# A streaming encoder step on one Trainium2 core: the head tables are made three pairs of blocks later, the planner is told of the weights' three places, and the weights' rounding is written behind a block's first step

## The chip, the core and the metric

The kernel runs on one core of one Trainium2 chip. Its engines run side by side, each through its own list of instructions in order: TensorE (PE in the profile) multiplies, VectorE (DVE), ScalarE (ACT) and GpSimd (POOL) do everything else, and SyncE (SP) issues most transfers. An engine whose next instruction waits for something stands still, with all that is queued behind it. The metric is the device time of one execution in microseconds.

## The reference

Two layers of an encoder run on 512 new frames and on 64 frames that continue a stream with 1024 cached frames; here they are 576 columns side by side. What matters of one layer:

```
h = rms_norm(x, norm_g);  proj = h @ w_in          # u, z, q, k, v, qi, ki, wi, z_a, g_p, g_a
br_pool = (pool_mix(u) * silu(z)) @ w_pool_out
q, k, qi, ki = rope(...)                           # rotary embedding
score = sum_h wi * relu(qi . ki);  keep the top 128 (new stream) or 256 (cached stream)
o = softmax(q k^T over the kept) v                 # 8 heads of 64
br_attn = (o * silu(z_a)) @ w_attn_out
x = x + (sigmoid(g_p) * br_pool + sigmoid(g_a) * br_attn) @ w_o
```

All of it is float32. The kernel reaches that accuracy with TensorE's faster fp32r format by splitting each operand in a rounded high part and the rest, and adding three products.

## The kernel before

**Blocks.** The weights come as 59 pieces of 128x1024 per layer. One piece makes one block: 8 steps of 6 matmuls over 288 columns (`step`, called by `product`, called by `block`). `ORDER` sets the blocks of a layer: 2 index queries, u0-u3 and z0-z3 (pooled branch), then four groups of two gates and one pooled output (gp0, gp1, po0, ..., gp6, gp7, po3), then k, q and v of four head pairs, za0-za3, ga0-ga7, four attention outputs and eight blocks wo0-wo7 of w_o.

**Weights.** SP loads a piece into one of three `raw` places. ScalarE writes the rounded part into the first half of a `whl` tile (three places) and minus the rounded part into the second half; GpSimd then issues a DMA that adds the raw piece to that second half (`split_to`). In block i `split_to(i + 3)` is written ahead of the block's matmuls, so ScalarE's two instructions for piece i+2 stand there. Their `whl` place is that of piece i-1, so they wait until TensorE has ended block i-1.

**Order.** The program is scheduled by hand: each engine's order is the order in which the code is written. A class `Plan` keeps for each engine the time at which it would be free by a table of costs. All work other than the blocks (attention units, transposes, selection) stands in generators. After every step `plan.pump()` asks which generator's next piece could run by the plan, and writes it there. So a cost or a wait that the plan does not know moves work to places where it is not ready. `Plan.slot` tells the plan when a place of a ring comes free for some rings, but not for `whl`.

**Head tables.** `head_tables()` loads the cosine and sine tables (two 288 KB loads on SP) into `tmp` tiles, and GpSimd multiplies each by the norm factors `Rt` into `Ct` and `St` (128x576 each). Blocks k and q use them. It is started at gp0.

**Attention.** For each head: logits into PSUM (`sm<-quart,qz` and `qzl`), minimum and mask on VectorE, exponential and normalising on ScalarE (`prob`), transposes on TensorE (`sm<-ident,prob`), rounding on ScalarE and rest on VectorE (`big`), values on TensorE (`sm<-big,quart`). PSUM has four `sm` places. The cached stream follows (`sample`): logits `sm<-big,qzs`, one exponential over 1088 columns, transposes `sm<-ident,quart`. In layer 0, block wo's output goes through `added`: two ScalarE instructions (rounded input of the next layer, square).

Of the kernel before, what the change touches and what calls it, by code (L numbers as in the profile page):

```python
# [11 lines left out]
F32R = mybir.dt.float32r  # L12
# [3 lines left out]
P = 128  # L16
# [30 lines left out]
UNITS = 3  # L47
FIRST_H = ()
LAG = (1, 2)
DMA_US = 3.0  # L50
WARM = 11
NORM_A = 0
# [12 lines left out]
class Plan:  # L65
# [77 lines left out]
    def run(self, eng, op, args, kw):  # L143
# [18 lines left out]
        if eng == "dma" or op == "dma_start":  # L162
            n = 1
            for k in outs[0].shape[1:]:
                n *= k
            late = DMA_US + 4 * outs[0].shape[0] * n / 180e3
        for x in outs:
# [48 lines left out]
    def start(self, gen, rank=1):  # L216
        item = [rank, len(self.todo), gen, None]
        self.todo.append(item)
        self.todo.sort(key=lambda x: x[0])
        self.step(item)  # L220
        return item
# [46 lines left out]
def encoder_step(ctx: ExitStack, tc: tile.TileContext, a: dict):  # L268
    nc = tc.nc
    plan = Plan()  # L270
# [5 lines left out]
    rot = ctx.enter_context(tc.tile_pool(name="rot", bufs=1))  # L276
# [7 lines left out]
    def tmp(n=T, dtype=F32):  # L284
        return rot.tile([P, 608], dtype, name="tmp", tag="tmp", bufs=NTMP)[:, :n]
# [16 lines left out]
    def ps_mm():  # L302
        return plan.slot("mm", 2, psum.tile([P, 2, 512], F32, name="mm", tag="mm", bufs=2), False)

    def ps_s(hold=False):
        return plan.slot("sm", 4, psum.tile([P, 512], F32, name="sm", tag="sm", bufs=4), hold)
# [22 lines left out]
    for l in range(DEPTH):  # L329
        pieces += [(l, j) for j in range(a["n_pieces"])]  # L330
    raw_of, split_of = {}, {}
    state = {"load": 0, "split": 0, "next": 0}

    def load_to(n):
        while state["load"] < min(n, len(pieces)):
            i = state["load"]
            l, j = pieces[i]
            raw_of[i] = raws()
            dma.dma_start(raw_of[i], a["w"][l, j])
            state["load"] += 1  # L340

    def split_to(n):
        while state["split"] < min(n, len(pieces)):
            i = state["split"]
            load_to(i + 1)
            x = raw_of.pop(i)
            w = rot.tile([P, 2, 1024], F32R, name="whl", tag="whl", bufs=3)
            act.copy(w[:, 0], x)

            act.activation(w[:, 1], x, AF.Copy, scale=-1.0)  # L350
            pool.dma_start(w[:, 1].bitcast(F32), x, accum_op=OP.add)
            plan.let(x)
            split_of[i] = w
            state["split"] += 1

    def split_first(i=0):

        load_to(i + 1)
        x = raw_of.pop(i)
        w = rot.tile([P, 2, 1024], F32R, name="whl", tag="whl", bufs=3)  # L360
        for c, eng in ((slice(0, 512), dve), (slice(512, 1024), pool)):
            act.copy(w[:, 0, c], x[:, c])
            eng.tensor_tensor(w[:, 1, c], x[:, c], w[:, 0, c].bitcast(F32), op=OP.subtract)
        plan.let(x)
        split_of[i] = w
        state["split"] = i + 1

    def weights():
        i = state["next"]
        state["next"] += 1  # L370
        split_to(i + 1)
        load_to(i + 4)
        w = split_of.pop(i)
        return w, i
# [60 lines left out]
    ps = ps_s()  # L435
# [3 lines left out]
    def step(ps, w, xh, xl, k, nk, off=0, parts=((0, 0, HT), (1, HT, T)), low=(False, True)):  # L439

        c = slice(off + k * P, off + (k + 1) * P)
        wh, wl = w[:, 0, c], w[:, 1, c]
        for s, t0, t1 in parts:
            cols = slice((k % 2) * T + t0, (k % 2) * T + t1)
            h, lo = xh[k // 2][:, cols], xl[k // 2][:, cols]
            o = ps[:, s, :t1 - t0]
            if False in low:  # L450
                pe.matmul(o, lhsT=wh, rhs=h, start=k == 0, stop=False)
                pe.matmul(o, lhsT=wh, rhs=lo, start=False, stop=False)
            if True in low:
                pe.matmul(o, lhsT=wl, rhs=h, start=False, stop=k == nk - 1)

    def product(ps, w, xh, xl, nk, off=0):
        for k in range(nk):
            step(ps, w, xh, xl, k, nk, off)
            plan.pump()

    def block(xh, xl, nk=8):
        w, i = weights()
        split_to(i + 3)
        ps = ps_mm()
        product(ps, w, xh, xl, nk)
        return ps

    class Entry:
# [29 lines left out]
        def first(self, k, x, ki_split):  # L498

            c = slice((k % 2) * T, (k % 2 + 1) * T)  # L500
            g = gains[:, self.l, k:k + 1]
            h = self.h[k // 2][:, c]
            if k in FIRST_H:
                dve.tensor_scalar(h, x, g, None, op0=OP.mult)
            else:
                act.activation(h, x, AF.Copy, scale=g)
            if k == 0:
                ki_split()
            dve.scalar_tensor_tensor(self.lo[k // 2][:, c], x, g, h.bitcast(F32), op0=OP.mult, op1=OP.subtract)
            self.rest.append(x)  # L510
            if k == 7:
                for i, x in enumerate(self.rest):
                    sq = tmp() if i else self.acc
                    act.activation(sq, x, AF.Square)
                    if i:
                        dve.tensor_tensor(self.acc, sq, self.acc, op=OP.add)
# [27 lines left out]
    def prepare_ki(l):  # L544
        rk = prob()
        rki = rk[:, :320].rearrange("p (k c) -> p k c", k=8)
        dma.dma_start(rk[:, :320], a["w_ki"][l])

        def ki_split():
            act.copy(kiw[:, :, 0:40], rki)  # L550
            (pool if l else dve).tensor_tensor(kiw[:, :, 64:104], rki, kiw[:, :, 0:40].bitcast(F32), op=OP.subtract)

        return ki_split

    def layer(l, x, arrive):
        xh, xl = x.h, x.lo
# [10 lines left out]
        w, n = weights()  # L567
        if l:
            split_to(n + 3)
# [8 lines left out]
        ps_k, ps_q0 = [ps_s(True) for _ in range(2)], ps_mm()  # L578
        lag = (0, 0) if l else LAG
        for k in range(8 + lag[1]):  # L580
# [30 lines left out]
        w, n = weights()  # L611
# [234 lines left out]

        def u_job(g):
            ps = block(xh, xl)
            ux = tmp(608)
            pool.memset(ux[:, 0:PST], 0.0)  # L850
# [96 lines left out]
        def po_job(m2):  # L947
            if m2 == 0:
                plan.finish(*mixes)
            w, n = weights()  # L950
            split_to(n + 3)
            for i in range(2):
                ps = ps_mm()
                product(ps, w, ah, al, 4, off=512 * i)
                pb = sgs.pop(2 * m2 + i)
                dve.tensor_tensor(halves(pb), ps[:, :, :HT], halves(pb), op=OP.mult)

                def go(pb=pb, m=2 * m2 + i):
                    yield lambda: need("dma", pb)
                    dma.dma_start(mp_d[l][m], pb)  # L960

                start(go(), 2)
            if m2 == 3:
                let(*ah, *al)
# [3 lines left out]
        def head_tables():  # L968
            Ct.append(rot.tile([P, T], F32, name="Ct", tag="acc", bufs=1))
            for raw, t in zip((table(2), table(3)), (Ct[0], St)):  # L970
                yield lambda: need("pool", raw)
                pool.tensor_tensor(t, raw, Rt, op=OP.mult)
# [150 lines left out]
        def attend():  # L1123
            yield lambda: {1, 2, 3} <= done
            for p in range(4):
                yield lambda: p in kv and p in q_there
                for e in range(2):
                    yield lambda: 2 * p + e < 2 + len(heads_done)
                    for j in (3, 2, 1, 0):
                        yield lambda: on_way[0] < UNITS and psum_free() and need("pe", kv[p], *qz[p]) and need("dve", room=ROOM)  # L1130
                        on_way[0] += 1
                        start(unit(p, e, j), 2)
                        logits_of[p] = logits_of.get(p, 0) + 1
                let(kv[p])
            let(macc)
            yield lambda: len(heads_done) == 8 and 4 in done
            yield from sample()
# [182 lines left out]
        for name, i in ORDER:  # L1320
            if name == "k" and i == 0:
                att = start(attend(), 3)
            if name == "gp" and i == 0:
                start(head_tables(), 2)
            jobs[name](i)
        plan.finish(sel)
# [14 lines left out]
        for m2 in range(4):  # L1341
            w, n = weights()
            split_to(n + 3)
            for i in range(2):
# [4 lines left out]
                ps = ps_mm()  # L1349
# [27 lines left out]
        for m in range(8):  # L1377
            residual(m + 1)
            if m == 3 and l + 1 < DEPTH:
                ki_split = prepare_ki(l + 1)  # L1380
# [4 lines left out]
            ps = block(mh, ml)  # L1385
# [57 lines left out]
        for s, t0, t1, starts in ((0, 0, CUT, (0, P, CUT - P)), (1, CUT, T, (CUT, T - P))):  # L1443
            for m in (6, 7):
                w, ps = wps[m - 6]
# [11 lines left out]
    ki_split = prepare_ki(0)  # L1457
# [7 lines left out]
    def arrive(k):  # L1465
        x.first(k, xt[k // 2][:, (k % 2) * T:(k % 2 + 1) * T], ki_split)
        if k == 7:
            plan.let(*xt)
        if k == 1:
            split_first()  # L1470
# [110 lines left out]
```

## Time and profile before

| | us |
|---|---|
| median of 3 runs | 920.47 (920.26 to 920.74) |
| the profiled execution | 921.1, its span 919.3 |
| TensorE busy | 894.8 (97% of the span) |
| VectorE busy | 668.3 (73%) |
| ScalarE busy | 593.2 (65%) |
| GpSimd busy | 202.1 (22%) |
| DMA by GpSimd's queue / by SP's queue | 59.78 MB / 100.08 MB |

The span runs from the first to the last instruction. Busy time of a pipelined TensorE counts a matmul from issue to result, longer than the distance at which the next may follow. "Idle before" in brackets is how long the engine stood still before the instruction, and what ended that.

### The profile page before, as it was taken

What the parts mean: (1) busy time and instruction counts of PE and PEld (TensorE: products, weight loads), DVE (VectorE), ACT (ScalarE), POOL (GpSimd) and SP (SyncE); (2) the same over time, 40 slices, a digit from 0 to 9 for tenths busy, and PEclk for the clock granted to TensorE, in tenths of its full rate; (3) what the DMA queues carried; (4) which work ended last, traced back from release to release, by engine and by line L of the source; (5) the groups of instructions that cost most, each with busy time, mean ns of one, the idle gap of its engine ahead of it and who ended that gap; (6) DMA issues with size and microseconds to landing.
All of it is one profiled execution on the core that took longest, in us unless ns stands there. A gap on an engine that the chain in (4) does not pass through costs nothing.

```text
span 919.3 us, 17403 instructions
## 1 busy us (share of the span) xinstructions
PE 894.8 (97%) x6613; PEld 881.4 (96%) x6613; DVE 668.3 (73%) x1554; ACT 593.2 (65%) x1056; POOL 202.1 (22%) x217
## 2 busy tenths in 40 slices
PE   8999999999999999999999999999999999999996
PEld 7999999999999999999999999999999999999995
DVE  6996899799896677362359779988989875755314
ACT  7556534588898975564537564446889988556642
POOL 3111211134432300112211121113443222011121
PEclk9999999999999999999999999999999999999998
DMA  7756587766555675779976667786655548648862
GB/s 266 187 140 164 134 214 189 173 161 160 125 145 147 179 199 150 186 202 240 263 191 175 154 151 163 191 203 180 165 139 133 157 124 221 189 135 222 236 146 104
DMA packets 54500, 160.97 MB, mean 175 GB/s; under 512 B 6736, under 2 KB 9040, under 8 KB 54416
## 3 DMA queue, kind: packets, MB, share of 16 engines
q0 software_dynamic: 16416, 59.78, 34.8%
q1 hardware_dynamic: 38000, 100.08, 32.2%
q8 instruction: 52, 0.85, 0.4%
q14 instruction: 32, 0.26, 0.1%
HBM read 85.37 MB, written 14.69 MB: 109 GB/s over the span
## 4 chain that ended last, share of the span: by engine, by line
PE 68%; DVE 14%; ACT 13%; issue 3%; DMA 1%; POOL 1%; SPq 0%; DVEq 0%; ACTq 0%; POOLq 0%
PE mm L262 57%; PE sm L262 11%; DVE tmp L262 6%; DVE quart L262 6%; ACT prob L262 4%; ACT whl L262 3%; ACT quart L262 2%; ACT qz L262 1%; ACT L262 1%; DVE big L262 1%; ACT tmp L262 1%; POOL tmp L262 1%; DMA raw<-in_w_dram 1%; DMA prob<-in_c_v_dram 1%; DVE prob L262 0%
## 5 line engine op out<-in xcount | busy, mean ns | idle before, releaser
L262 PE MATMUL mm<-quart,whl 128*128 128x288 f32 (+1 forms) x5568 | 780.4, 296 | 1.6 <-ACT quart L262 1.2
L262 PEld LDWEIGHTS mm<-quart,whl 128*128 128x128 f32 x5568 | 754.2, 188 | 4.3 <-ACT quart L262 2.0
L262 POOL DMA_DIRECT2D whl<-raw x114 | 99.3, 871 | 648.9 <-ACT whl L262 433.1
L262 ACT CAST whl<-raw 128x1024 fp32r<-128x1024 f32 (+1 forms) x118 | 121.8, 1034 | 133.2 <-PE mm L262 88.7
L262 ACT ACTIVATE whl<-raw 128x1024 fp32r<-128x1024 f32 x114 | 120.4, 1056 | 0.0
L262 ACT ACTIVATE prob<-prob,stat 128x128 f32<-128x128 f32 (+3 forms) x128 | 67.5, 554 | 6.8 <-DVE stat L262 6.4
L262 DVE SCALAR_TENSOR_TENSOR quart<-prob,wcol,quart 128x256 f32<-128x256 f32 (+4 forms) x60 | 42.1, 704 | 26.4 <-ACT prob L262 25.1
L262 ACT ACTIVATE prob<-sm 128x256 f32<-128x256 f32 (+4 forms) x72 | 33.5, 481 | 38.4 <-PE sm L262 38.4
L262 DVE MATCH_REPLACE8 quart<-stat,quart 128x256 f32<-128x256 f32 (+2 forms) x96 | 51.1, 539 | 0.0
L262 DVE MAX8 stat<-quart 128x8 f32<-128x256 f32 (+2 forms) x96 | 47.3, 541 | 0.0
L262 DVE MAX8 quart<-quart 128x8 f32<-128x544 f32 x64 | 46.3, 723 | 1.2
L262 DVE MATCH_REPLACE8 quart<-quart 128x544 f32<-128x544 f32 x64 | 45.4, 709 | 0.0
L262 DVE TENSOR_TENSOR tmp<-tmp 128x576 f32<-128x576 f32 (+7 forms) x62 | 44.3, 720 | 1.3
L262 DVE TENSOR_TENSOR quart<-quart 128x576 fp32r<-128x576 f32 (+6 forms) x30 | 26.4, 881 | 21.5 <-ACT quart L262 21.0
L262 DVE TENSOR_TENSOR big<-sm,big 128x512 fp32r<-128x512 f32 (+1 forms) x64 | 28.9, 483 | 16.3 <-ACT big L262 16.1
L262 ACT CAST quart<-tmp 64x512 fp32r<-64x512 f32 (+4 forms) x44 | 24.1, 566 | 22.0 <-POOL tmp L262 11.7
L262 ACT COPY prob<-sm 64x512 f32<-64x512 f32 (+1 forms) x24 | 12.3, 514 | 39.0 <-PE sm L262 38.6
L262 PE MATMUL sm<-quart,big 128*128 128x128 f32 (+3 forms) x176 | 32.2, 291 | 1.4 <-DVE tmp L262 1.4
L262 ACT CAST big<-sm 128x512 fp32r<-128x512 f32 (+2 forms) x72 | 28.0, 434 | 8.4 <-PE sm L262 8.0
L262 DVE SCALAR_TENSOR_TENSOR quart<-tmp,gains,quart 128x576 fp32r<-128x576 f32 x8 | 6.5, 818 | 31.6 <-ACT quart L262 31.6
L262 DVE CUSTOM_DVE_ANT_0 prob<-sm,quart 128x512 f32<-128x512 f32 (+2 forms) x48 | 25.8, 550 | 4.8 <-PE sm L262 4.8
L262 DVE TENSOR_TENSOR quart<-mm,tmp 128x576 f32<-128x576 f32 (+2 forms) x10 | 6.4, 638 | 29.3 <-PE mm L262 29.3
(157 smaller groups left out, 1025.5 us busy)
## 6 DMA issues: line engine op xcount, KB each, us to landing
raw<-in_w_dram SPq DMA_DIRECT2D x116, 512.0 KB, 4.9
whl<-raw POOLq DMA_DIRECT2D x114, 512.0 KB, 4.8
mp<-tmp SPq DMA_DIRECT2D x16, 288.0 KB, 3.3
tmp<-mp SPq DMA_DIRECT2D x16, 288.0 KB, 4.7
prob<-in_c_k_dram SPq DMA_DIRECT2D x16, 256.0 KB, 4.8
prob<-in_c_v_dram SPq DMA_DIRECT2D x16, 256.0 KB, 3.8
out_o_v_dram<-quart SPq DMA_DIRECT2D x8, 320.0 KB, 4.6
quart<-in_x_dram SPq DMA_DIRECT2D x8, 288.0 KB, 6.3
```

The source lines that it names most:

```text
L262: return f(*args, **kw)
```

## The change

Four edits. (1) A `whl` tile of piece i > 2 is now told to the plan as free only when the last use of piece i-3's tile ends (`whls`). (2) In `block`, `split_to(i + 3)` is called by `product` after step 0 and its pump, not ahead of the block. The blocks po and the attention outputs keep it ahead. (3) `head_tables()` starts at gp6 in place of gp0. (4) In `first`, for the first 128 rows of x, the rounding of the small index weights `kiw` is written ahead of x's own rounding on ScalarE.

```
+TABLES_AT = 6
+SPLIT_AT = 0
...
+    def whls(i):
+
+        w = rot.tile([P, 2, 1024], F32R, name="whl", tag="whl", bufs=3)
+        whl_names.append(w.tensor.name)
+        if i > 2:
+            plan.wrote(w, plan.last[whl_names[i - 3]])
+        return w
...
-            w = rot.tile([P, 2, 1024], F32R, name="whl", tag="whl", bufs=3)
+            w = whls(i)
...
-    def product(ps, w, xh, xl, nk, off=0):
+    def product(ps, w, xh, xl, nk, off=0, ahead=0):
         for k in range(nk):
             step(ps, w, xh, xl, k, nk, off)
             plan.pump()
+            if k == SPLIT_AT:
+                split_to(ahead)
 
     def block(xh, xl, nk=8):
         w, i = weights()
-        split_to(i + 3)
         ps = ps_mm()
-        product(ps, w, xh, xl, nk)
+        product(ps, w, xh, xl, nk, ahead=i + 3)
         return ps
...
             else:
+                if k == 0:
+                    ki_split()
                 act.activation(h, x, AF.Copy, scale=g)
-            if k == 0:
-                ki_split()
...
-            if name == "gp" and i == 0:
+            if name == "gp" and i == TABLES_AT:
                 start(head_tables(), 2)
```

What the plan makes of it shows in the order. GpSimd's list in layer 0, from the end of the u blocks on (a `DMA whl<-raw` is the adding DMA of one piece), before:

```order
L262 MEMSET tmp 128x15
L262 DMA whl<-raw 128x1024 x5
L262 TENSOR_TENSOR Ct<-tmp,Rt 128x576
L262 TENSOR_TENSOR St<-tmp,Rt 128x576
L262 DMA whl<-raw 128x1024 x13
```

and in the changed kernel:

```order
L264 MEMSET tmp 128x15
L264 DMA whl<-raw 128x1024 x14
L264 TENSOR_TENSOR Ct<-tmp,Rt 128x576
L264 TENSOR_TENSOR St<-tmp,Rt 128x576
L264 DMA whl<-raw 128x1024 x4
```

The two products stand behind nine more pieces: behind po3's in place of po0's.

TensorE's list in layer 0 where the cached stream begins (`sm<-big,qzs` are its logits, `sm<-ident,quart` the transposes of its first head pair), before:

```order
L262 MATMUL mm<-quart,whl 128x288 x36
L262 MATMUL sm<-big,qzs 128x364 x6
L262 MATMUL sm<-big,qzs 128x360 x3
L262 MATMUL mm<-quart,whl 128x288 x30
L262 MATMUL sm<-ident,quart 128x128 x4
L262 MATMUL mm<-quart,whl 128x288 x6
```

and in the changed kernel:

```order
L264 MATMUL mm<-quart,whl 128x288 x36
L264 MATMUL sm<-big,qzs 128x364 x6
L264 MATMUL sm<-big,qzs 128x360 x3
L264 MATMUL mm<-quart,whl 128x288 x48
L264 MATMUL sm<-ident,quart 128x128 x4
L264 MATMUL sm<-big,qzs 128x364 x6
```

Between the logits and the transposes that wait for the exponential there are now 48 matmuls of the blocks, and were 30.

ScalarE's list at the start of layer 0's blocks wo (after the table load: two instructions of `split_to` for each `CAST whl`; `quart<-tmp,gains` and `acc<-tmp` are `added` of the first output block), before:

```order
L262 ACT_TABLE_LOAD
L262 ACTIVATE scratch<-ones 128x1
L262 CAST whl<-raw 128x1024
L262 ACTIVATE whl<-raw 128x1024
L262 CAST whl<-raw 128x1024
L262 ACTIVATE whl<-raw 128x1024
L262 ACTIVATE quart<-tmp,gains 128x576
L262 ACTIVATE acc<-tmp 128x576
```

and in the changed kernel:

```order
L264 ACT_TABLE_LOAD
L264 ACTIVATE scratch<-ones 128x1
L264 CAST whl<-raw 128x1024
L264 ACTIVATE whl<-raw 128x1024
L264 ACTIVATE quart<-tmp,gains 128x576
L264 ACTIVATE acc<-tmp 128x576
L264 CAST whl<-raw 128x1024
L264 ACTIVATE whl<-raw 128x1024
```

The second piece's rounding now stands behind the two instructions of `added`, and so on in the following blocks.

## Rows read from the trace of the kernel before

**Rows 1.** The page: span, and busy time of each engine.
```profile
span 919.3 us, 17403 instructions
...
PE 894.8 (97%) x6613; PEld 881.4 (96%) x6613; DVE 668.3 (73%) x1554; ACT 593.2 (65%) x1056; POOL 202.1 (22%) x217
```

**Rows 2.** Busy time by stretch: stretch, length, engines' busy us, clock, DMA share, GB/s.
```profile
200.00:300.00 100.00, 97.94 (x725) 95.53 (x724) 84.90 (x222) 87.31 (x194) 37.70 (x36) 1.00 0.56 144
300.00:400.00 100.00, 97.84 (x737) 96.66 (x737) 63.31 (x146) 68.54 (x112) 13.74 (x15) 1.00 0.69 183
...
600.00:700.00 100.00, 98.02 (x726) 96.39 (x725) 87.50 (x210) 75.37 (x151) 33.70 (x33) 1.00 0.63 162
700.00:800.00 100.00, 97.89 (x725) 96.20 (x724) 75.10 (x199) 83.40 (x165) 24.77 (x24) 1.00 0.65 171
```

**Rows 3.** Timeline, gp1 of layer 0: start us, us, instruction, idle before.
```profile
93.94 1.75 POOL L262 TENSOR_TENSOR Ct<-tmp,Rt 128x576 f32<-128x576 f32 x1
94.07 3.56 DVE L262 SCALAR_TENSOR_TENSOR quart<-prob,wcol,quart 128x512 f32<-128x512 f32 x1 [1.80 <-ACT prob L262]
...
95.34 1.73 POOL L262 TENSOR_TENSOR St<-tmp,Rt 128x576 f32<-128x576 f32 x1
...
98.97 0.50 PE L262 MATMUL sm<-quart,big 128*128 128x512 f32 x1 [0.70 <-DVE tmp L262]
...
99.26 0.74 DVE L262 SCALAR_TENSOR_TENSOR quart<-prob,wcol,quart 128x512 f32<-128x512 f32 x1
```

**Rows 4.** Timeline, the same wait in layer 1.
```profile
547.31 0.50 PE L262 MATMUL sm<-quart,big 128*128 128x512 f32 x1 [0.73 <-DVE tmp L262]
```

**Rows 5.** Timeline of POOL and DVE, v0 and k1 of layer 0.
```profile
208.59 1.30 POOL L262 TENSOR_TENSOR quart<-quart 128x512 fp32r<-128x512 f32 x1
...
208.78 0.73 DVE L262 MAX8 quart<-quart 128x8 f32<-128x544 f32 x1
```

**Rows 6.** Timeline, where the cached stream begins, layer 0.
```profile
330.44 4.15 PE L262 MATMUL mm<-quart,whl 128*128 128x288 f32 x30
...
331.43 1.05 ACT L262 CAST whl<-raw 128x1024 fp32r<-128x1024 f32 x1 [3.12 <-PE mm L262]
...
333.34 1.19 ACT L262 ACTIVATE quart<-quart,stat 128x1088 f32<-128x1088 f32 x1
...
335.78 0.63 PE L262 MATMUL sm<-ident,quart 128*128 128x128 f32 x4 [1.20 <-DVE quart L262]
```

**Rows 7.** Timeline, last unit of the new stream's attention, layer 0.
```profile
318.75 1.03 ACT L262 CAST whl<-raw 128x1024 fp32r<-128x1024 f32 x1
...
321.09 0.33 PE L262 MATMUL sm<-ident,prob 128*128 128x128 f32 x1 [0.81 <-ACT prob L262]
```

**Rows 8.** Timeline of ACT and PE, q1 to k2 of layer 0.
```profile
199.94 1.61 ACT L262 ACTIVATE prob<-prob,stat 128x512 f32<-128x512 f32 x3
...
202.12 0.93 PE L262 MATMUL sm<-ident,prob 128*128 128x128 f32 x7
...
218.83 0.62 ACT L262 COPY tmp<-mm 128x576 f32<-128x576 f32 x1
...
219.50 0.77 PE L262 MATMUL sm<-ident,tmp 128*128 128x128 f32 x5 [0.91 <-ACT tmp L262]
```

**Rows 9.** Timeline of PE and ACT, blocks wo0 to wo3 of layer 0.
```profile
404.76 30.53 PE L262 MATMUL mm<-quart,whl 128*128 128x288 f32 x227
...
413.81 1.05 ACT L262 CAST whl<-raw 128x1024 fp32r<-128x1024 f32 x1 [0.32 <-ACT whl L262]
...
423.99 1.05 ACT L262 CAST whl<-raw 128x1024 fp32r<-128x1024 f32 x1 [6.93 <-DMA raw<-in_w_dram]
```

**Rows 10.** Busy time by stretch, layer 0's blocks wo (columns as in rows 2).
```profile
436.00:440.00 4.00, 4.00 (x31) 3.87 (x30) 0.55 (x1) 3.25 (x4) 0.85 (x1) 1.00 0.98 304
```

**Rows 11.** The tile whl: the adding DMAs, issue to landing.
```profile
DMA to landing us min/median/max: 4.5/4.8/10.4
```

**Rows 12.** Timeline, the first weights at the start.
```profile
8.21 1.14 ACT L262 CAST whl<-raw 128x512 fp32r<-128x512 f32 x2 [1.25 <-DMA raw<-in_w_dram]
```

More of the change, by code (lines that the diff above doesn't have):

```diff
@@ L331, in encoder_step @@
     raw_of, split_of = {}, {}
+    whl_names = []
     state = {"load": 0, "split": 0, "next": 0}
@@ L359, in split_first @@
         x = raw_of.pop(i)
-        w = rot.tile([P, 2, 1024], F32R, name="whl", tag="whl", bufs=3)
+        w = whls(i)
         for c, eng in ((slice(0, 512), dve), (slice(512, 1024), pool)):
```

## The prediction

> **What bounds the kernel now.** The page comes first: TensorE is busy 97% of the span, the next engine 73% [rows 1]. So the kernel is bound by TensorE's list, and an edit pays only where it removes time in which TensorE stands still, or costs only where it adds some. Next I read busy time by stretch [rows 2]. From 100 on TensorE's idle time lies almost wholly in the attention stretches: 2.06, 2.16, 1.98 and 2.11 us in the four shown, 8.31 together. The granted clock is 1.00 in all of them, so the clock is no part of this. The timelines of these stretches then name each wait.
>
> What does a wait cost? 30 matmuls fill 4.15 us before a wait [rows 6], 227 fill 30.53 without one [rows 9]. If matmuls follow each other at a pitch p, and the last one of a row counts longer by e, then 29p+e = 4.15 and 226p+e = 30.53, so p = 0.134 and e = 0.27. Before a wait the row thus ends about 0.14 to 0.16 after the next matmul could have started; I add 0.16 to the idle time shown. The 8.31 us stand in some 20 waits, and cost about 11.5 us.
>
> **Head tables, -1.75.** Before, GpSimd makes `Ct` and `St` from 93.94 and 95.34 [rows 3]. VectorE's product of `prob`, `wcol` and `quart`, 0.74 us when alone at 99.26, takes 3.56 us at 94.07 and ends at 97.63, just behind `St` (97.07). So VectorE was held for 2.82 us by both products, and at 98.97 TensorE waits 0.70 us for a PSUM place that VectorE has not read out. Layer 1 shows 0.73 [rows 4]. Removed, these are 0.86 + 0.89 = 1.75 us.
>
> The products are not gone: they stand behind po3's adding DMA now. There VectorE runs the selection, whose instructions read one SBUF operand. Such a pair can be seen before: a `MAX8` over 544 columns took 0.73 us inside a GpSimd product of 1.30 us [rows 5], which is no longer than the 0.74 us of the undisturbed product over 512 columns [rows 3]. So I put the move itself at nothing; if VectorE were held there as at gp1, the whole 1.75 would come back. The two loads move too, on SP's queue behind the weights' loads. From gp6's end to block k0, where the tables are first read, lie two blocks of 48 matmuls, 12.9 us at p; the kernel's DMAs onto `whl` land in at most 10.4 [rows 11]. Behind the products on GpSimd stand the adding DMAs of the next pieces, which have the slack worked out below.
>
> The Trainium skill, "SBUF — State Buffer", section "Who interferes with whom", has VectorE and GpSimd share a port pair, locked for one whole instruction; a VectorE instruction with two SBUF inputs contends with a GpSimd one that reads SBUF, one with a single SBUF input does not. The second half agrees with rows 5; by the first half VectorE's product would have waited for `Ct` alone and ended near 96.4, and the row's 97.63 says otherwise. By the rule alone the tables term would be 0, since 1.2 us less delay is more than the wait of 0.70.
>
> **The cached stream's exponential, -2.72.** At 331.43 ScalarE starts the rounding of a weight piece after standing still for 3.12 us until TensorE freed its place; the exponential over 1088 columns is queued behind it and its second half, and runs at 333.34, 1.91 us later. TensorE's transposes then wait 1.20 us [rows 6]. Costed: (1.20 + 0.16) x 2 layers = 2.72. The planner put the rounding there since it took the place for free. Told of the places, it has 48 matmuls between logits and transposes in place of 30: 18 x 0.134 = 2.4 us more cover, against 1.2 missing. So I take the whole; the bounds are 0 (the exponential still behind a waiting cast) and 2.72.
>
> **The last unit's normalising, -1.94.** At 318.75 a cast and its second half stand ahead of the last normalising, and the transposes wait 0.81 us for `prob` [rows 7]. In the new order this unit's transposes stand more than a block's length behind its logits. (0.81 + 0.16) x 2 = 1.94, bounds 0 and 1.94.
>
> **Waits from k1 to k3, -0.8.** Here all of the order is reshuffled, and this is the least certain term. Before, the transposes of v1 wait 0.91 for a copy that ends at 219.45 [rows 8]; with five smaller ones the stretch from 200 to 300 is idle for 2.06 us [rows 2], which costs 3.0. In the new order the copy has about 41 matmuls (5.5 us) as cover, where it had 24 (3.2 us), so this wait and the one that follows from it go, about 1.5 us. But the first nine transposes of a head stand 12 matmuls (1.6 us) earlier: at 200.5 in place of 202.12, while the normalises that they need run from 199.94 to 201.55, 0.54 each [rows 8]. The first is ready in time, the rest follow at 0.54 where a transpose takes 0.13, so a new wait of some 0.35 us; I count two more like it, of about 0.35 each, where GpSimd's chain for v1's and k2's heads comes close. Net -1.5 + 1.1 = -0.4 per layer. Bounds for both layers: all old waits gone and none new, -6.0; old waits kept and new ones added, +2.2.
>
> **Weights rounded later, +1.0.** A cast that stood at a block's head now comes after step 0 and what the planner writes there: one or two ScalarE instructions over 576 columns (0.62 for one such [rows 8]), so 0.8 (6 matmuls) to 2.1 us later. Its slack: from a block's head to the piece's first matmul are two blocks, 12.9 us; the cast and its second half take 1.9 (331.43 to 333.34 [rows 6]), landing typically 4.8 [rows 11]. Some 6 us are left, so 2.1 us cost nothing where DMA is not crowded. It is crowded in layer 0's blocks wo: there the DMA share is 0.98 [rows 10], landing takes up to 10.4, and 12.9 - 1.9 - 10.4 leaves 0.6, less what stands between (the first piece there is already just in time: 227 matmuls run on without a wait [rows 9]). wo3's cast at 413.81 would now come about 2.1 us later, behind `added`; I charge half of that, 1.0, as the later pieces' casts wait there for their raw load (6.93 us at 423.99 [rows 9]), not for ScalarE's list. Bounds 0 and 2.1; more is a rival.
>
> **The first weights, 0.** Edit 4 lets the small index weights go ahead. But at 8.21 ScalarE waits 1.25 us for the raw piece [rows 12]: the first blocks are held by that load, with or without the edit. If not, about 0.5 us either way.
>
> **The sum.** -1.75 - 2.72 - 1.94 - 0.8 + 1.0 = -6.2. The profiled execution took 921.1; so 914.9 profiled. The median of the runs lies 0.6 below it, hence 914.3.
>
> **The rivals.**
> - *Less: new waits for old.* The planner's list only moves: the pieces that are rounded later wait at other places ahead of other exponentials. Then only the tables' gain is left, 920.5 - 1.75 = 918.7. For it: every unit's place changes, and ScalarE is 75 to 87% busy in the stretches from 200 and 600 [rows 2], so a cast will stand ahead of something. Against it: rows 6 show a cast that waited 3.12 us ahead of the exponential, which a planner that knows of the place has no reason to write.
> - *More: the attention waits all go.* 8.31 us idle, 11.5 with the 0.16 each: 920.5 - 11.5 - 1.75 + 1.0 = 908.2. Against it: most waits of 0.3 us are for VectorE's `big` or the GpSimd chain, which no edit speeds.
> - *One lock, one instruction.* VectorE's product was not held by both products, its lateness has another source, and the tables' waits stay: 916.1. Against it: the end at 97.63 behind `St` [rows 3]; the rule of the Trainium skill quoted above would have it so.
> - *Slower: the weights of layer 0's last blocks.* DMA is nearly full there [rows 10], so a landing that starts later is not caught up: each of the six blocks wo2 to wo7 would lose the 2.1 us by which its rounding moves, 12.6 us against a gain of 7.2: 920.5 - 7.2 + 12.6 = 925.9. It decides from 7.2 us lost there. Against it: from wo4 on the casts wait for raw loads [rows 9], and what is now written ahead of them can run in that idle time.
>
> **How the numbers follow.** Chances: forecast 0.55, less 0.18, more 0.12, one lock 0.05, slower 0.10. The forecast's own range is 911 to 917.5, from the k1-to-k3 bounds cut to what is likely and one term of 2 to 3 us that fails. The range of 909.5 to 919.5 takes in the rival of less and part of that of more, and leaves out the slower one and the deep end. A measurement here tells about 0.2% (1.8 us) from no change: faster means below 918.6. Half of "less" lies on either side of that, so with 0.02 of the forecast: faster 0.79, same 0.12, slower 0.09.
>
> **What would show it.** Tables: the product at gp1 back at 0.74 and no wait ahead of `sm<-quart,big`; VectorE not held at po3. Exponential: no cast between the mask and the exponential of 1088, and no wait ahead of `sm<-ident,quart`. Normalising: no 0.8 us wait for `prob`. In all, TensorE's idle time from 200 to 400 and 600 to 800 below 8.3, about 5. Wrong would be: new waits for `prob` or `quart` in k1 to k3 above 1 us, TensorE waiting for `whl` from 404 to 450 or in the pooled branch, or a wait for `Ct` at k0.

## The result, and the profile after

The changed kernel takes 909.13 us (908.18 to 910.61), the kernel before in the same sitting 920.61 (920.26 to 921.6): a ratio of 0.9875, 95% interval 0.9858 to 0.9892, or 11.5 us less. Forecast were 914.3 and a range of 909.5 to 919.5, so the sign was right, the size was not, and the time lies just below the range, near the rival of *more* (908.2).

The page of the profiled execution, which took 908.79:

```profile
span 907.0 us, 17415 instructions
...
PE 891.8 (98%) x6613; PEld 881.7 (97%) x6613; DVE 662.7 (73%) x1554; ACT 594.1 (65%) x1056; POOL 200.0 (22%) x217
```

The span is 12.3 us shorter than before [rows 1], with the same 6613 matmuls. Busy time by stretch, columns and stretches as in [rows 2]:

```profile
200.00:300.00 100.00, 99.83 (x740) 97.68 (x740) 92.32 (x250) 90.95 (x204) 33.39 (x33) 1.00 0.53 137
300.00:400.00 100.00, 100.00 (x760) 99.63 (x759) 59.05 (x123) 68.75 (x107) 17.79 (x18) 1.00 0.77 205
600.00:700.00 100.00, 99.85 (x739) 97.92 (x738) 88.58 (x224) 83.70 (x174) 33.54 (x33) 1.00 0.62 157
700.00:800.00 100.00, 100.00 (x753) 99.07 (x752) 79.06 (x199) 81.50 (x156) 23.11 (x22) 1.00 0.65 170
```

TensorE's idle time in the four attention stretches falls from 8.31 us to 0.32. I had expected about 5 to be left. Now the single places. First gp1 and po3 of layer 0, VectorE and GpSimd:

```profile
95.54 0.75 DVE L264 SCALAR_TENSOR_TENSOR quart<-prob,wcol,quart 128x512 f32<-128x512 f32 x1 [2.20 <-ACT prob L264]
...
153.90 1.77 POOL L264 TENSOR_TENSOR Ct<-tmp,Rt 128x576 f32<-128x576 f32 x1
155.30 1.75 POOL L264 TENSOR_TENSOR St<-tmp,Rt 128x576 f32<-128x576 f32 x1
...
155.19 0.68 DVE L264 MATCH_REPLACE8 quart<-stat,quart 128x512 f32<-128x512 f32 x1
155.78 0.88 DVE L264 MAX8 stat<-quart 128x8 f32<-128x256 f32 x2
```

VectorE's product is back at 0.75 from 3.56 [rows 3], and the selection beside the two moved products is not held (0.68 for 512 columns; all 32 of this kind take 0.675 in the mean). Next the last unit's transpose and the cached stream, TensorE and ScalarE, and the blocks wo of layer 0:

```profile
305.95 0.27 PE L264 MATMUL sm<-ident,prob 128*128 128x128 f32 x1
...
317.85 6.55 PE L264 MATMUL mm<-quart,whl 128*128 128x288 f32 x48
...
320.58 1.21 ACT L264 ACTIVATE quart<-quart,stat 128x1088 f32<-128x1088 f32 x1
...
324.23 0.60 PE L264 MATMUL sm<-ident,quart 128*128 128x128 f32 x4
...
403.73 36.56 PE L264 MATMUL mm<-quart,whl 128*128 128x288 f32 x273
```

The transpose at 305.95 has no wait in brackets, where 0.81 stood [rows 7], and neither have those at 324.23, where 1.20 stood [rows 6]. From 403.73 on 273 matmuls run in 36.56 us, 0.134 each: in this execution no weight piece is waited for. Last, k1 to k3, TensorE and ScalarE:

```profile
199.34 1.61 ACT L264 ACTIVATE prob<-prob,stat 128x512 f32<-128x512 f32 x3
...
200.10 1.34 PE L264 MATMUL sm<-ident,prob 128*128 128x128 f32 x9
...
208.33 0.33 PE L264 MATMUL sm<-ident,prob 128*128 128x128 f32 x1
...
218.94 0.63 ACT L264 COPY tmp<-mm 128x576 f32<-128x576 f32 x1
...
221.68 0.71 PE L264 MATMUL sm<-ident,tmp 128*128 128x128 f32 x5
```

ScalarE's copy for v1 runs at 218.94, no sooner than before (218.83 [rows 8]). But TensorE comes to the transposes that need it at 221.68 in place of 219.50, and has worked on the next head's logits, transposes and values meanwhile. This wait has gone because TensorE's list has more in front of it, not because ScalarE is faster.

### The profile page after: what moved, and what is told of

The parts are those of the page before. It is cut to its first block, busy times and chain, and to the rows that moved or that the text cites. A ratio compares the mean times of both kernels' runs of the same rounds, so it can differ in the third digit from the quotient of the medians.

```text
span 907.0 us, 17415 instructions
## 1 busy us (share of the span) xinstructions
PE 891.8 (98%) x6613; PEld 881.7 (97%) x6613; DVE 662.7 (73%) x1554; ACT 594.1 (65%) x1056; POOL 200.0 (22%) x217
## 4 chain that ended last, share of the span: by engine, by line
PE 88%; DVE 6%; ACT 4%; issue 1%; POOL 1%; DMA 1%; SPq 0%; DVEq 0%; POOLq 0%; ACTq 0%
PE mm L264 73%; PE sm L264 14%; DVE tmp L264 3%; DVE quart L264 2%; ACT prob L264 1%; ACT quart L264 1%; POOL tmp L264 1%; DMA quart<-in_x_dram 1%; ACT whl L264 1%; ACT qz L264 0%; ACT L264 0%; ACT tmp L264 0%; SPq L264 0%; DVE rcol L264 0%; DVE acc L264 0%
## 5 line engine op out<-in xcount | busy, mean ns | idle before, releaser
L264 ACT ACTIVATE prob<-prob,stat 128x256 f32<-128x256 f32 (+3 forms) x128 | 67.7, 556 | 4.7 <-DVE stat L264 4.2
L264 DVE SCALAR_TENSOR_TENSOR quart<-prob,wcol,quart 128x256 f32<-128x256 f32 (+4 forms) x60 | 36.4, 609 | 28.6 <-ACT prob L264 27.5
L264 DVE TENSOR_TENSOR tmp<-tmp 128x576 f32<-128x576 f32 (+7 forms) x62 | 42.4, 688 | 1.3
L264 DVE TENSOR_TENSOR tmp<-mm,tmp 128x576 f32<-128x576 f32 x28 | 21.0, 750 | 29.4 <-PE mm L264 29.2
L264 ACT COPY prob<-sm 64x512 f32<-64x512 f32 (+1 forms) x24 | 12.3, 512 | 34.8 <-PE sm L264 34.6
L264 ACT ACTIVATE tmp<-quart 128x576 f32<-128x576 f32 (+2 forms) x24 | 14.4, 639 | 22.3 <-DVE quart L264 22.3
```

The source lines that it names most:

```text
L264: return f(*args, **kw)
```

## The experiments

Two kinds were made: each edit alone on the kernel before, and each edit taken out of the changed kernel. In the second kind the lines of that edit stand as on the minus side of the change's diff.

**Each edit alone.** The kernel before takes 920.72 beside these. Head tables:

```
+TABLES_AT = 6
...
-            if name == "gp" and i == 0:
+            if name == "gp" and i == TABLES_AT:
```

> The kernel before with edit 3 alone (head tables started at gp6). TensorE's, VectorE's and ScalarE's lists are those of before; GpSimd's two products stand behind po3's adding DMA. Theory of the prediction: VectorE's product at gp1 is back at 0.74 us, both waits of 0.70 and 0.73 ahead of sm<-quart,big are gone, nothing new at po3: 920.6 - 1.75 = 918.9. Rival (one lock covers one instruction, the waits have another source): the waits stay, 920.6.

Measured: 919.05 us, ratio 0.9980 (0.9971 to 0.9989), 1.7 less. VectorE's product at gp1:

```profile
94.09 0.75 DVE L264 SCALAR_TENSOR_TENSOR quart<-prob,wcol,quart 128x512 f32<-128x512 f32 x1 [1.79 <-ACT prob L264]
```

As the prediction's theory has it: the term of 1.75 stands.

The places of `whl`:

```
+    def whls(i):
...
+        if i > 2:
+            plan.wrote(w, plan.last[whl_names[i - 3]])
...
```

> The kernel before with edit 1 alone (the plan knows the places of whl). Theory of the prediction (the places are what frees the exponential and the normalising): -2.72 - 1.94, so 916.0 or less. Rival (the rounding's place in the block does it): from the order, the cast of ga5's piece still stands ahead of the exponential, with the logits 6 matmuls later; the exponential is late by 1 us in place of 1.9, and TensorE's wait falls from 1.20 to about 0.35 in each layer, the 0.81 for the last normalising stays, and k1 to k3 are as before: about 918.9.

Measured: 919.72 us, ratio 0.9984 (0.9976 to 0.9993), 1.0 less. The prediction's theory falls: 4.7 were promised. The rival is nearer, but not right either. ScalarE and TensorE where the cached stream begins, and TensorE further on:

```profile
330.15 1.05 ACT L264 CAST whl<-raw 128x1024 fp32r<-128x1024 f32 x1 [0.83 <-PE mm L264]
...
332.55 1.21 ACT L264 ACTIVATE quart<-quart,stat 128x1088 f32<-128x1088 f32 x1 [0.39 <-DVE stat L264]
...
335.45 0.60 PE L264 MATMUL sm<-ident,quart 128*128 128x128 f32 x4
...
351.73 0.77 PE L264 MATMUL sm<-big,qzs 128*128 128x364 f32 x3 [0.20 <-DVE big L264]
353.12 1.10 PE L264 MATMUL sm<-big,qzs 128*128 128x364 f32 x5 [0.63 <-DVE big L264]
```

The cast still stands ahead of the exponential, but does not delay it any more (it waits 0.39 for VectorE's minimum now), and the 1.20 is gone. But 18 us later the next head pair's logits wait 0.20 and 0.63 for VectorE's `big`, which gives most of it back. The rival had k1 to k3 as before; there the 0.91 for v1's copy is gone too, and in its place TensorE waits 0.85 us at 196.93 for VectorE's `stat`. The wait for the last normalising is untouched.

The rounding behind step 0:

```
         for k in range(nk):
             step(ps, w, xh, xl, k, nk, off)
             plan.pump()
+            if k == SPLIT_AT:
+                split_to(ahead)
...
         w, i = weights()
-        split_to(i + 3)
...
```

> The kernel before with edit 2 alone (split_to after step 0). TensorE's and VectorE's lists are then those of the changed kernel, word for word. Theory (the rounding's place in the block gives the attention's gain, without the places): TensorE's waits from 200 to 400 and from 600 to 820 nearly all go, about 5.1 us in each layer, the tables' 1.75 stay: 920.6 - 10.3 = 910.3. Rival (the places are needed): at least the 1.20 ahead of sm<-ident,quart and the 0.81 ahead of sm<-ident,prob stay, above 915.

Measured: 910.99 us, ratio 0.9893 (0.9878 to 0.9908), 9.7 less. This one edit carries nearly all. The first two attention stretches, and the tables' wait that is left:

```profile
200.00:300.00 100.00, 99.87 (x740) 97.54 (x740) 92.32 (x251) 90.97 (x203) 33.34 (x33) 1.00 0.54 138
300.00:400.00 100.00, 100.00 (x759) 99.63 (x759) 59.10 (x122) 69.06 (x108) 17.76 (x18) 1.00 0.77 203
```
```profile
91.79 0.50 PE L264 MATMUL sm<-quart,big 128*128 128x512 f32 x1 [0.60 <-DVE tmp L264]
```

The start:

```
+                if k == 0:
+                    ki_split()
                 act.activation(h, x, AF.Copy, scale=g)
-            if k == 0:
-                ki_split()
```

> The kernel before with edit 4 alone (kiw rounded ahead of x). Theory (the start is won, then lost to the clock): the index products and first blocks run 1.1 us earlier, as in the changed kernel, the wait ahead of sm<-ones,acc grows by 0.7 us, and the granted clock falls in 24 to 28 (0.70 and 0.50 in the changed kernel), which costs about 1.5: 920 to 921. Rival (the fall of the clock belongs to another edit): 1.1 less the 0.7, clock 1.00 in 20 to 40, 920.2. Rival (edit 4 does nothing at all): 920.6, and the first product at 6.87 as before.

Measured: 920.59 us, ratio 1.0001 (0.9993 to 1.0010). TensorE's first products, and the clock behind them:

```profile
5.99 1.97 PE L264 MATMUL sm<-quart,kiw 128*128 128x288 f32 x8
```
```profile
10.00:12.00 2.00, 1.37 (x6) 1.37 (x7) 2.00 (x4) 2.00 (x3) 0.00 (x0) 0.65 1.05 416
12.00:14.00 2.00, 2.00 (x10) 2.00 (x10) 1.49 (x3) 0.75 (x2) 0.00 (x0) 0.50 1.03 414
```

The products start 0.9 us sooner than before (6.87), and nothing of it shows in the time. In this execution the granted clock falls at 10 to 14, not at 24 to 28 as in the changed kernel; more on that below.

**Each edit taken out.** The kernel before takes 921.29 beside these.

> The changed kernel without edit 3: head tables started at gp0 again. Theory (GpSimd's products hold VectorE wherever it has an instruction with two SBUF operands): the product of prob, wcol and quart at gp1 takes some 3.5 us again, and TensorE waits 0.7 there in each layer: 909.1 + 1.75 = 910.9. Rival (in the new order another, shorter instruction meets them, and the cover is enough): 909.1.

Measured: 911.28 us, ratio 0.9891 (0.9877 to 0.9904), where the whole change has 0.9875. In the new order another instruction of VectorE meets the products, with 384 columns:

```profile
86.94 1.76 POOL L264 TENSOR_TENSOR Ct<-tmp,Rt 128x576 f32<-128x576 f32 x1
88.33 1.75 POOL L264 TENSOR_TENSOR St<-tmp,Rt 128x576 f32<-128x576 f32 x1
```
```profile
86.96 3.54 DVE L264 SCALAR_TENSOR_TENSOR quart<-prob,wcol,quart 128x384 f32<-128x384 f32 x1 [1.71 <-ACT prob L264]
```

It takes 3.54 in place of 0.61, and TensorE waits 0.60. The time agrees with the theory, but the two intervals overlap; the trace decides it.

> The changed kernel without edit 1: the plan takes whl's places for free again. The order differs from the changed kernel's by one exponential of 364 columns on ScalarE in each layer. Theory (edit 1 adds nothing to edit 2): 909.1, within 0.5. Rival (the places carry the exponential's and normalising's gain): 909.1 + 4.7 = 913.8.

Measured: 908.67 us, ratio 0.9860 (0.9847 to 0.9874). Without edit 1 the kernel is as fast as with it; that it looks 0.15% faster is within the intervals. TensorE's, VectorE's, GpSimd's and SyncE's lists are the same with and without edit 1, once edit 2 is there.

> The changed kernel without edit 2: split_to stands ahead of the block again. Theory (edit 2 carries the gain): only the tables and what the places give alone are left: 920.6 - 1.75 - 1.7 = 917.2. Rival (edit 1 carries it): 920.6 - 1.75 - 4.7 = 914.2 or less.

Measured: 918.36 us, ratio 0.9969 (0.9956 to 0.9981). Edits 1, 3 and 4 together give 2.9 us. The wait for the last normalising is back (1.78 in layer 1):

```profile
320.27 0.33 PE L264 MATMUL sm<-ident,prob 128*128 128x128 f32 x1 [0.80 <-ACT prob L264]
```

> The changed kernel without edit 4: kiw rounded behind x's first instruction. Theory (edit 4 wins 1.1 us at the start and loses as much to the granted clock and a longer wait at 21 to 23): first product at 6.87, clock 1.00 in 20 to 40, 908.5 to 909.5. Rival (edit 4 is a gain): 909.1 + 0.4 to 1.1. Rival (the clock's fall is from edit 2's order): the fall stays and 1.1 is lost, 910.2.

Measured: 909.73 us, ratio 0.9871 (0.9857 to 0.9884), the same as the whole change. In its profiled execution the clock stays at 1.00 from 20 to 40, but it shows a loss of another kind, TensorE and ScalarE in layer 0's blocks wo:

```profile
441.57 2.66 PE L264 MATMUL mm<-quart,whl 128*128 128x288 f32 x18 [1.58 <-DMA whl<-raw]
```
```profile
431.71 1.05 ACT L264 CAST whl<-raw 128x1024 fp32r<-128x1024 f32 x1 [2.60 <-DMA raw<-in_w_dram]
```

A raw load came late, its cast waited 2.60 us for it, and TensorE 1.58 for the piece. The changed kernel's profile has the same lists there and no such wait (the 273 matmuls above), so this differs from execution to execution. It is not alone: the execution without edit 3 waits 0.88 us at 441.67, behind a cast that waited 2.42 for its raw load, and 0.25 in layer 1's wo. So two of the five profiled executions with edit 2 show late pieces in wo, and none of the six with the rounding as before.

**What holds VectorE.** `Ct` at gp0 as before, `St` at gp6, on the kernel before:

```
-        def head_tables():
...
-            for raw, t in zip((table(2), table(3)), (Ct[0], St)):
+        def head_tables(n):
...
+            raw, t = table(2 + n), (Ct[0], St)[n]
...
-            if name == "gp" and i == 0:
-                start(head_tables(), 2)
+            if name == "gp" and i in (0, 6):
+                start(head_tables(i // 6), 2)
```

> The kernel before with the head tables split: Ct's load and product at gp0 as before, St's at gp6. Theory (VectorE stays held as long as GpSimd's products follow each other): its product of prob, wcol and quart at gp1 is held by one product only and takes 1.7 to 2.0 us in place of 3.56; that is 1.6 less, more than the wait of 0.70, so TensorE's two waits go and the time is that of the kernel with edit 3 alone, 919.0. Rival (VectorE's instruction is slow there for another reason): 3.5 us and 920.7.

Measured: 919.71 us beside 921.25, ratio 0.9987 (0.9972 to 1.0002): 1.5 less by the medians, not clear of no change by the interval. The trace is clear:

```profile
94.54 1.75 POOL L262 TENSOR_TENSOR Ct<-tmp,Rt 128x576 f32<-128x576 f32 x1
```
```profile
94.66 2.19 DVE L262 SCALAR_TENSOR_TENSOR quart<-prob,wcol,quart 128x512 f32<-128x512 f32 x1 [1.79 <-ACT prob L262]
```

VectorE's product takes 2.19 with one of GpSimd's beside it (1.7 to 2.0 were expected), 3.56 with two in a row, 0.74 with none, and TensorE's wait ahead of `sm<-quart,big` is gone.

**How late the rounding may be.** The changed kernel with another step in one line (1 here, then 3 and 5), beside 921.25:

```
-SPLIT_AT = 0
+SPLIT_AT = 1
```

> The changed kernel with split_to after step 1 in place of step 0: roundings 0.8 us later, and a new order in the attention. Theory (rounding behind the planner's pieces is what helps, and 0.8 us is within what the blocks wo can bear once or twice): 909 to 911, TensorE waits for whl in layer 0's wo by at most 1 us. Rival (each block from wo2 to wo7 loses the delay): 909.1 + 6 x 0.8 = 914.

Measured: 917.66 us, ratio 0.9958 (0.9942 to 0.9974). Both expectations missed it. One step later costs most of the gain, and not in wo. TensorE in layer 0's attention:

```profile
322.16 1.07 PE L264 MATMUL mm<-quart,whl 128*128 128x288 f32 x6 [0.55 <-DMA whl<-raw]
```
```profile
351.38 1.03 PE L264 MATMUL sm<-big,qzs 128*128 128x364 f32 x4 [1.07 <-DVE quart L264]
```

In the two stretches from 200 to 400 TensorE is idle for 0.66 and 1.91 us again.

> The changed kernel with split_to after step 3: roundings 2.4 us later. Slack of the pieces for wo2, wo3 and wo5 in the changed kernel is 0.2 to 0.4 us. Theory (one late landing is paid once, since from wo4 the casts wait for their raw loads): 2 to 3 us of waits for whl in layer 0's wo, 911 to 912.5. Rival (each of six blocks loses it): 909.1 + 6 x 2 = 921.

Measured: 919.89 us, ratio 0.9979 (0.9969 to 0.9989). Missed again, and again for the attention. TensorE there, and in layer 0's blocks wo:

```profile
270.34 0.44 PE L264 MATMUL sm<-ident,prob 128*128 128x128 f32 x2 [1.84 <-ACT prob L264]
```
```profile
399.83 40.43 PE L264 MATMUL mm<-quart,whl 128*128 128x288 f32 x302
```

With roundings 2.4 us later 302 matmuls in layer 0's wo run in 40.43 us, 0.134 each: no weight is late there in this execution. In layer 1's wo TensorE waits 0.54 for one piece, at 886.26.

> The changed kernel with split_to after step 5: roundings 4.0 us later. Theory (paid once or twice in wo, nearly nothing where landing takes 4.8 and 5 us are spare): 3.6 to 7 us of waits for whl, 913 to 916. Rival (each of six blocks): 909.1 + 6 x 3.7 = 931.

Measured: 935.14 us, ratio 1.0157 (1.0137 to 1.0178). Both expectations missed it. This kernel does not compute the same as the others: the pooled branch's states, two of the ten outputs, come out as not-a-number. So it is read for its waits only. What TensorE waited for: what ended the wait, us in total, times, longest.

```profile
PE mm L264 <- DMA whl<-raw: 9.0, 9, 2.2
PE sm L264 <- ACT tmp L264: 5.0, 5, 2.2
PE sm L264 <- ACT prob L264: 2.9, 6, 1.0
```

At 4 us the weights are late, nine times, all of them ahead of the blocks wo, none in wo.

## Why the prediction was wrong

**The step that failed: "Waits from k1 to k3, -0.8".** I took off 1.5 us per layer for the old waits and put 1.1 back for new ones. From 200 to 300 the idle time fell from 2.06 us [rows 2] to 0.17, from 600 to 700 from 1.98 to 0.15. With 0.16 for each of some four waits gone in each layer the two are 2.5 and 2.5 us, 5.0 in place of 0.8. Two things were wrong in it. The nine transposes that stand 12 matmuls sooner hardly wait for the normalises (0.17 us is all the idle time left from 200 to 300), since these run 0.6 us sooner too (199.34 in place of 199.94 [rows 8]). And I kept all small old waits, though the reshuffled lists left none of them of 0.15 us or more. My own lower bound for this term, -6.0, was the better number: the rival of *more* took it, and I gave it 0.12 with the argument that no edit speeds `big` or GpSimd's chain. The argument fails, since an order moves both ends of a wait. At v1's copy TensorE comes later. At the logits that waited 0.19 us for `big` at 206.00, `big` comes sooner: the transposes ahead of it do (200.10 in place of 202.12), and two instructions of the selection no longer stand ahead of it on VectorE. VectorE before, and in the changed kernel:

```profile
205.18 1.47 DVE L262 TENSOR_TENSOR big<-sm,big 128x512 fp32r<-128x512 f32 x3
```
```profile
203.13 1.49 DVE L264 TENSOR_TENSOR big<-sm,big 128x512 fp32r<-128x512 f32 x3
```

That the rival's 908.2 comes so near is in part luck: its 11.5 us for all waits counts some 20 of them, where the timelines name 13 of 0.15 us or more and some 10.2 us went, and its +1.0 for the weights does not show in the profiled execution.

**"Weights rounded later, +1.0": 0 in the profiled execution.** No piece is late in layer 0's wo there (273 matmuls without a wait), nor with the rounding 2.4 us later. I charged wo3 for the one longest landing, 10.4 us [rows 11], as if a later cast had to meet it; there it did not. But two of the five executions with edit 2 do wait in wo, 1.58 and 0.88 + 0.25 us, for pieces whose casts waited for late raw loads, and none of six without it. That was among my signs of being wrong. Whether the later rounding makes these loads late is not shown. It costs little on the whole, since the other terms make 12.0 and the median is 11.5 lower. The slower rival falls: no execution loses 2.1 us in each of six blocks. What I had not looked at is that late weights can hurt in the attention (0.55 at 322.16 with step 1).

**"The cached stream's exponential, -2.72" and "the last unit's normalising, -1.94".** Both waits went, and the idle time from 300 to 400 and 700 to 800 with them: 2.16 and 2.11 to nothing. With three waits of 0.16 in each layer this is 5.2 in place of 4.66; the rest is a wait for `quart` at the second head pair, which I had not counted. But the cause was named wrongly: I wrote "Told of the places, it has 48 matmuls". Edit 1 alone removes the exponential's 1.20 and gives most of it back 18 us later; it leaves the normalising. Edit 2 alone removes both, and with it edit 1 moves nothing but one exponential of 364 columns. The order could have shown this beforehand: built with edit 2 alone, TensorE's list is word for word that of the whole change. I had looked at the order of the whole change only.

Of edit 2 itself, what matters is the pump between step 0 and the rounding. With the rounding written behind step 0 but ahead of the pump, all five lists come out the same as without edit 2 (this was read from the order, it was not run). So the pieces of attention work that are ready at a block's start have to go in front of the two rounding instructions, nearly 2 us of ScalarE. That this is good at step 0, and not at steps 1 and 3, is what their runs show: they get other lists with other waits. Why just this list has nearly no wait is not explained by a rule; it was found, and its neighbours were not as good.

**"Head tables, -1.75": right.** 1.7 us alone; the waits are gone, nothing came back at po3. The section "Who interferes with whom" of the page "SBUF — State Buffer" in the Trainium skill has one instruction hold the port pair that VectorE and GpSimd share; the run with one product agrees with that (2.19, ending 0.56 behind `Ct`), but with two in a row VectorE is not let in between (3.56 in the kernel before, 3.54 without edit 3), and the measurement decides. The rival of one lock falls.

**"The first weights, 0": right in size.** The reason given, the raw load, was not it: in the changed kernel that cast waits 0.48 in place of 1.25, and TensorE runs 0.8 to 1.1 us ahead up to 21. It loses this again to the wait for `acc` at 22.64 (0.94, before 0.23 at 23.03) and to the clock (below): at 37.69 it is 0.4 behind the kernel before (37.27).

**The sum** by these: -1.75 - 5.0 - 5.2 + 0 + 0 = -12.0, against a span shorter by 12.3 and a median lower by 11.5. With the 0.4 lost at the start, the rest of the span is 12.7 shorter, of which 0.7 is not accounted for. The runs of the changed kernel spread over 2.4 us; the clock at the start and now and then a late raw load in wo are what the profiles show of this, and that they are all of it is not shown. The profiled one is 0.3 below the median.

## What to carry to other kernels

When a change moves the order of a hand-scheduled program, compare the lists with each edit alone before costing anything: they tell which edit owns which move. Price a reshuffled stretch from both ends, and weigh the end where all old waits go: here it was the better number (-6.0, against 5.0 measured). And take a good order as a find: one step further in one line gave back two thirds of it.

## What was not expected of the hardware

**VectorE is held by GpSimd's instructions as a row.** An instruction of VectorE with two operands in SBUF that met two products of GpSimd in a row took 3.56 us, one product 2.19, none 0.74; it was not let in between the two.

**The clock at the start.** In the changed kernel's profiled execution TensorE waits 0.94 us at 21.7 to 22.6, and then the granted clock stands at 0.60 in the mean over 24 to 28, that is partly at the lower of its levels, 1.2 GHz:

```profile
24.00:28.00 4.00, 4.00 (x22) 3.99 (x22) 1.52 (x9) 1.22 (x3) 1.43 (x2) 0.60 1.02 195
```

Only 22 matmuls run there, where the kernel before, at 1.00, has 32; ten matmuls are 1.3 us at 0.134 each. But it does not belong to edit 4: with the start as before the profiled executions show 1.00 there (the kernel before, the changed one without edit 4) or 0.68 (edit 1 alone), and with edit 4 alone the fall comes at 10 to 14, as shown above. Nor is the wait enough for it: in the execution with one product TensorE waits 1.06 us for `acc`, and the clock is 1.00 from 24 to 28. What decides it stays open.
